# Sums of two adaLN vectors on VectorE, 256 columns of both at a time, instead of 32-column products

## The chip, the cores and the metric

The kernel runs on one core of one Trainium2 chip. Time is that of the device for one execution, in microseconds (us). Five engines work beside each other and wait for one another by semaphores: TensorE (PE in the profile, its weight loads PEld), VectorE (DVE), ScalarE (ACT), GpSimd (POOL) and SyncE (SP), which here issues the loads of weights.

## The reference

Two blocks of two layers each work on 256 tokens of 1024 features, the first one with 256 context tokens beside them. What matters here is how the layers of the first block are steered: a vector `c` (and a second one, `c_ctx`, for the context) gives shift, scale and gate through one product with `w_ada` of 1024 x 3072.

```python
sc = jax.nn.silu(c)                 # 1024 numbers
sc_ctx = jax.nn.silu(c_ctx)         # 1024 numbers
for l in range(2):
    shift, scale, gate = split((sc @ w_ada[l] + b_ada[l]), 3)
    shift_c, scale_c, gate_c = split(sc_ctx @ w_ada[l] + b_ada[l], 3)
    h  = rmsnorm(x, norm_w) * (1 + scale) + shift
    hc = rmsnorm(ctx, norm_w) * (1 + scale_c) + shift_c
    ...                             # h @ w_in; mLSTM, difference attention and Fourier branch; merge
    x = x + gate * merge(...)
    ctx = ctx + gate_c * merge(...) # first layer only
```

So each column of `w_ada` is summed twice, once with the weights of `silu(c)` and once with those of `silu(c_ctx)`. The second block (window attention, block attention, MLP) has only one such vector for each layer.

## The kernel before

All big products run in float32, with each operand split into a high and a low part and three products (high x high, high x low, low x high) for each 128 rows of the contraction. Weights come as tiles of 128 x 1024 numbers (512 KB) through nine slots w, loaded from a queue of SP. For each tile ACT makes the high part and DVE the low part (`w<-w,w`), and PE then works on it for some 24 products of 512 columns. Of raw tiles, that is loaded and not yet split or summed, five may wait (`NR`).

The kernel's program is written out at build time by a planner. It walks through the products stage by stage (in the first layer: the projections W, U, cz and bz, then the merge stages M00 to M31, four weight tiles each) and keeps a clock for each engine. Between two products it puts in "side work": attention steps, evacuations, splits and the adaLN sums, when by its clocks their operands are there and ACT and DVE are not too far ahead. A stage can name groups of side work that must be done before it starts (`need=`): U3 needs the attention's groups of its first unit, bz0 those of the second. What is left of them is then put in all at once by `plan.drain`, with no products between. Engines execute in the order that the planner wrote.

Tiles of `w_ada` are loaded between the other weight tiles (`stream.ada(..., rate=...)`). A chunk is 512 columns of `w_ada`, in four tiles. The chunks that matter here are

- the four of `mod1`, scale and shift of the second layer of the first block, loaded between the tiles of the stages from U1 on (in the trace their products with `stat` stand between 468.7 and 638.1), in use from layer 1 on;
- the two of the first layer's gates, group `gate0`, loaded from W24 on. They are applied by `ada_gate`, whose `use` waits for `have`, which says that the slot for the finished gates has come free (at the start of stage M30, in `pre_out`).

Each such tile goes to PE: four products of 32 x 256 with a block of `stat`, in which the two vectors stand among zeros (`p<-w,stat`), summed in PSUM over the chunk's four tiles. ACT copies the sum to the tile `acc`. For `mod1` (`ada_feat`) two small products against constants (`p<-cst,acc` of 128x8) bring the sums into columns, and for the gates (`ada_gate`) products of `acc` with a constant (`p<-acc,cst`) spread the row over all 128 partitions; DVE adds these to the bias that a DMA has put in place.

Chunks with one vector alone (the second block's, and the first block's last gate) already take another way, `ada_vec`: DVE multiplies the tile by a column of `stat` and adds it to `acc`, 512 columns at a time; PE sums over the partitions by a product with ones (`ada_rows`), ACT copies, a transpose makes columns, and DVE adds the bias. The tile `acc` has one buffer: `G("acc", 1)`.

Of the kernel before, what the change touches and what calls it, by code (L numbers as in the profile page):

```python
# [11 lines left out]
ALU = mybir.AluOpType  # L12
# [41 lines left out]
CALM, CALM2 = 750, 750  # L54
# [7 lines left out]
C_ID, C_SC, C_CS, C_Z, C_AL = 0, 128, 136, 652, 655  # L62
# [7 lines left out]
INF = float("inf")  # L70
# [3 lines left out]
class Bank:  # L74
# [3 lines left out]
    def __init__(self, *deps, n=1):  # L78
        self.deps, self.n = deps, n
# [503 lines left out]
def _build(tc, a, out, es):  # L583
    plan = Planner(lambda i: lp.tile([128, 512], F32, name=f"p{i}", tag=f"p{i}"), 3, 4)
# [38 lines left out]
    def expect(group, n=1):  # L623
        plan.pending[group] = plan.pending.get(group, 0) + n

    def fin(group):
        plan.pending[group] -= 1


    cst = cp.tile([128, NCST], F32, name="cst")  # L630
# [4 lines left out]
    ones = cp.tile([128, 128], F32, name="ones")  # L635
# [4 lines left out]
    def C(name, i=0, n=1):  # L640
        o = _COLS[name] + i
        return col[:, o:o + n]


    stat = cp.tile([128, 60], F32, name="stat")
# [34 lines left out]


    def ada_run(ch, stream):
        if ch["vec"] is not None:
            return ada_vec(ch, stream)

        def gen(_):
            prev = ch["prev"]
            over = lambda: INF if prev and not prev.get("over") else 0.0
            first = lambda: INF if prev and not prev.get("summed") else 0.0

            def there(q):
                return lambda: plan.gate([stream.raw[ch["idx"][q]]]) if q in ch["idx"] else INF
            ps = yield Bank(there(0), first)
            for q in range(4):
                if q:
                    yield [there(q)]
                elif "pre" in ch:
                    ch["pre"]()
                i = ch["idx"][q]
                r = stream.raw.pop(i)  # L700
                for par in range(2):
                    for half in range(2):
                        g = 32 * (2 * par + half)
                        nc.tensor.matmul(ps[g:g + 32, 0:256], stat[:, 4 * (2 * q + par):4 * (2 * q + par) + 32],
                                         r[:, 512 * par + 256 * half:512 * par + 256 * half + 256],
                                         start=(q == 0), stop=(q == 3))
                stream.drop(r)
            ch["summed"] = True
            yield [ps, over]
            sb = G("acc", 1)[:, 0:256]  # L710
            nc.scalar.activation(sb, ps[:, 0:256], AF.Copy)
            plan.release(ps)
            yield from ch["use"](sb)
            ch["over"] = True
        return gen

    def ada_vec(ch, stream):
# [31 lines left out]
            ch["over"] = True  # L749
        return gen  # L750

    def chunk(w, group, use, vec=None):
        expect(group)
        ch = dict(w=w, group=group, vec=vec)
        if isinstance(use, tuple):
            use, ch["pre"] = use
        ch["use"] = use
        return ch
# [44 lines left out]
    def ada_row(dst, brow):  # L803
# [9 lines left out]
            nc.gpsimd.dma_start(dst.rearrange("a (f n) -> (a f) n", f=4), acc[0:128:32, 0:128])  # L813
        return use, start

    def ada_gate(dsts, brow, wait):

        ds = {}

        def load():  # L820
            if not ds and wait() == 0.0:
                ds.update(dsts())
                for d in ds.values():
                    nc.gpsimd.dma_start(d, brow.to_broadcast([128, 512]))

        def use(sb):
            yield [wait]
            load()
            for m, d in ds.items():
                ps = yield Bank(sb, d)  # L830
                for half in range(2):
                    o = C_SC + 4 * half + m
                    nc.tensor.matmul(ps[:, 256 * half:256 * half + 256], cst[:, o:o + 1].to_broadcast([128, 128]), sb,
                                     start=True, stop=True)
                yield [ps]
                nc.vector.tensor_tensor(d, ps, d, ALU.add)
                plan.release(ps)
        return use, load

    class Mod:  # L840

        def __init__(self, group, w, bias, b0, norm, ms):
            self.ok = [0] * 4
            self.m = self.A = None
            self.ms, self.norm, self.group = ms, norm, group
            one = len(ms) == 1
            use = ada_cols if one else ada_feat
            self.chunks = [chunk((lambda q, c=c: w(c, q)), group,  # L850
                                 use((lambda c=c: self.dst(c)), C(bias, b0 + 4 * c, 4), lambda c=c: self.fin(c)),
                                 ms[0] if one else None)
                           for c in ((0, 2, 1, 3) if one else range(4))]

        def dst(self, c):
            n = len(self.ms)
            if self.A is None:
                b = 2 if n > 1 else 4
                self.A = cp.tile([128, n, 8], F32, name=f"modA{n}", tag=f"modA{n}", bufs=b)
                self.S = cp.tile([128, n, 8], F32, name=f"modS{n}", tag=f"modS{n}", bufs=b)  # L860
                if n > 1:
                    self.m = cp.tile([128, 2, 8, 3], F32, name="mod", tag="mod")
            if n > 1:
                return self.m[:, :, 2 * c:2 * c + 2, :]
            return (self.S, self.A)[c // 2][:, 0, 4 * (c % 2):4 * (c % 2) + 4]

        def fin(self, c):

            if self.m is not None:
                k0, n, qs = 2 * c, 2, (c,)  # L870
            else:
                k0, n, qs = 4 * (c % 2), 4, (2 * (c % 2), 2 * (c % 2) + 1)
            k = slice(k0, k0 + n)
            for q in qs:
                self.ok[q] += 1 if self.m is None else 2
            if self.ok[qs[0]] < 2:
                return
            for i, m in enumerate(self.ms):
                scale = self.A[:, i, k] if self.m is None else self.m[:, 1, k, m]
                nc.vector.scalar_tensor_tensor(self.A[:, i, k], scale, 1.0, C(self.norm, k0, n), ALU.add, ALU.mult)  # L880
                if self.m is not None:
                    nc.vector.tensor_copy(self.S[:, i, k], self.m[:, 0, k, m])
# [74 lines left out]
    stream = Stream(nc, plan, lambda i, dt: wp.tile([128, 1024], dt, name=f"w{i}", tag=f"w{i}"), mm, ada_run)  # L957
# [430 lines left out]
    def layer1(l, X, norm, ada_next, begin_out, on_token):  # L1388
# [317 lines left out]
        have = lambda: 0.0 if "gate" in st else INF  # L1706
        for c in range(2):
            gemm(W(24 + c), 8, 512, feats(vq, nx), ev_mc(c), pre=None if c else pre_mc,
                 need=() if c or last else ("cc",))
            if c == 0 and not last:  # L1710
                stream.ada(*[chunk((lambda q, c=c: a["wada"][l, 4 + c, q]), f"gate{l}{c}",
                                   ada_gate((lambda c=c: {m: st["gate"][:, m, 512 * c:512 * c + 512]
                                                          for m in range(2)}),
                                            a["bgate"][l:l + 1, 512 * c:512 * c + 512], have)) for c in range(2)],
                           front=True, rate=RATE["gate"])
                stream.ada(rate=RATE["mid"])
        if last:
# [142 lines left out]
    do(start_0)  # L1860


    mod1 = Mod("ada1", lambda c, q: a["wada"][1, c, q], "bada1", 0, "norm1", (0, 1))
    norm1 = Norm("h1", range(4), mod1, lambda t: 0 if t in (0, 3) else 1)

    def begin_1():
# [380 lines left out]
    n0, b0 = norm_of(0, mods[0][0])  # L2247
# [8 lines left out]
def _chunks(w, width=512):  # L2256

    import numpy as np
    K, N = w.shape
    kq = 1024 // width  # L2260
    v = w.reshape(K // (128 * kq), kq, 128, N // width, width).transpose(3, 0, 2, 1, 4)
    return np.ascontiguousarray(v).reshape(N // width, K // (128 * kq), 128, 1024)
# [31 lines left out]
def layout(inp):  # L2294
    import numpy as np
    g = {k: np.asarray(v) for k, v in inp.items()}
    d = {}
# [17 lines left out]
    win, wg, wmix, wada = [], [], [], []  # L2315
    win2, wkv2, wo2, wout2, wup2, wdn2, wada2 = [], [], [], [], [], [], []
    for l in range(2):
# [18 lines left out]
        w = g["w_in"][l]  # L2336
        o = np.cumsum([0, 512, 512, 1024, 16, 1024, 1024, 1024, 1024, 1024, 1024, 1024, 1024, 3072])
# [16 lines left out]
        w = g["w_ada"][l]  # L2354

        w = np.concatenate([w[:, :2048].reshape(1024, 2, 4, 256).transpose(0, 2, 1, 3).reshape(1024, 2048), w[:, 2048:]], 1)
        wada.append(_chunks(w))
        w = g["w_in_2"][l]
        o = np.cumsum([0, 512, 128, 128, 512, 512, 512, 1024, 1024])
        p = [w[:, o[i]:o[i + 1]] for i in range(8)]  # L2360
# [33 lines left out]
```

## Time and profile before

| | |
|---|---|
| runs | 2292.09, 2286.84, 2292.26 us; median 2292.09 |
| the profiled execution | 2286.09 us |
| its span in the profile | 2284.3 us |
| PE busy | 2242.7 us, 98% |
| PEld (weight loads, beside PE) | 1901.5 us, 83% |
| DVE busy | 1484.3 us, 65% |
| ACT busy | 1107.0 us, 48% |
| POOL busy | 269.0 us, 12% |

Busy time is the time in which at least one instruction of an engine was under way. Instructions of one engine overlap a little, so that the time from one start to the next is what counts in a row of them. A product in full float32 leaves two records, and so the profile's counts for these are twice those of the program.

### The profile page before, as it was taken

Reading aid. Unit: us, or ns where it says so; the run is one execution under the profiler, and the core shown is the slowest. Engines: PE = TensorE matmul, PEld = TensorE weight load, DVE = VectorE, ACT = ScalarE, POOL = GpSimd, SP = SyncE. Lnnn points to the kernel's source line nnn. Section 1 sums busy time; section 2 is a strip of 40 time slices with the busy share of each in tenths; the row PEclk is TensorE's granted clock in tenths of the full one; section 3 lists DMA queues with packets and bytes.
Section 4 is the critical chain, followed back from the end, with each engine's and each line's share of the span. In section 5 each row is a group of like instructions: output and inputs, shape, how many; then the busy total and the mean of one; then the engine's idle time right before and its main releaser. Section 6 shows DMA issues by size and latency. Waiting matters only on the chain. (4 is left out here: it accounts for less than half of the span.)

```text
span 2284.3 us, 34929 instructions
## 1 busy us (share of the span) xinstructions
PE 2242.7 (98%) x13228; PEld 1901.5 (83%) x13228; DVE 1484.3 (65%) x2856; ACT 1107.0 (48%) x2125; POOL 269.0 (12%) x439
## 2 busy tenths in 40 slices
PE   8999999999999999999999999999999999999999
PEld 6877888877777877878898888997998987798987
DVE  4667744457676734686975877678666656758554
ACT  4345322235565423435542556556655645656653
POOL 1012000014121000010200322003000002100000
PEclk9999999999999999999999999999999999999999
DMA  7443443353323453465674423464354564345454
GB/s 291 148 152 107 133 162 120 129 171 115 102 93 102 139 193 123 146 203 196 227 266 138 145 90 120 164 206 151 103 188 168 181 213 161 113 139 207 153 193 148
DMA packets 99913, 359.79 MB, mean 158 GB/s; under 512 B 11960, under 2 KB 12272, under 8 KB 99744
## 3 DMA queue, kind: packets, MB, share of 16 engines
q1 hardware_dynamic: 96192, 348.34, 44.9%
q0 software_dynamic: 3552, 9.22, 1.6%
q8 instruction: 104, 1.70, 0.3%
q14 instruction: 65, 0.53, 0.1%
HBM read 354.31 MB, written 3.20 MB: 157 GB/s over the span
## 5 line engine op out<-in xcount | busy, mean ns | idle before, releaser
L318 PE MATMUL mm<-h,w 128*128 128x256 f32 (+1 forms) x4048 | 819.4, 319 | 2.0 <-ACT qr L318 1.0
L318 DVE TENSOR_TENSOR w<-w,w 128x1024 fp32r<-128x1024 f32 x452 | 552.5, 1222 | 401.2 <-ACT w L318 354.3
L318 ACT ACTIVATE w<-w 128x1024 fp32r<-128x1024 f32 x461 | 486.6, 1058 | 667.0 <-PE mm L318 598.7
L318 PEld LDWEIGHTS mm<-h,w 128*128 128x128 f32 x4048 | 602.8, 190 | 61.2 <-issue 13.8
L318 PE MATMUL mm<-w,h 128*128 128x512 f32 (+1 forms) x1584 | 472.0, 392 | 10.3 <-DVE w L318 7.3
L318 PE MATMUL mm<-hl,w 128*128 128x512 f32 (+1 forms) x1040 | 354.2, 341 | 0.0
L318 PEld LDWEIGHTS mm<-w,h 128*128 128x128 f32 x1584 | 286.3, 190 | 79.4 <-DVE w L318 11.7
L318 PE MATMUL mm<-s,w 128*128 128x256 f32 (+1 forms) x1536 | 256.7, 326 | 0.6 <-DVE s L318 0.6
L318 PEld LDWEIGHTS mm<-s,w 128*128 128x128 f32 x1536 | 224.1, 190 | 25.3 <-issue 3.0
L318 PE MATMUL mm<-w,s 128*128 128x512 f32 x996 | 240.1, 391 | 0.0
L318 PE MATMUL mm<-w,hl 128*128 128x512 f32 (+1 forms) x608 | 231.5, 381 | 0.0
L318 PEld LDWEIGHTS mm<-w,s 128*128 128x128 f32 x996 | 186.2, 188 | 38.5 <-issue 0.4
L318 PEld LDWEIGHTS mm<-hl,w 128*128 128x128 f32 x1040 | 197.4, 190 | 20.8 <-issue 2.9
L318 DVE SCALAR_TENSOR_TENSOR acc<-w,stat,acc 128x512 f32<-128x512 f32 x192 | 143.7, 748 | 47.2 <-DMA w<-in_wada_dram 40.7
L318 PEld LDWEIGHTS mm<-w,hl 128*128 128x128 f32 x608 | 114.8, 189 | 22.2 <-DVE hl L318 0.2
L318 ACT ACTIVATE s<-mm 128x512 f32<-128x512 f32 (+2 forms) x142 | 67.3, 481 | 63.1 <-PE mm L318 62.9
L318 PE MATMUL p<-s 64*128 64x256 f32 (+3 forms) x464 | 85.7, 390 | 3.0 <-DVE s L318 1.5
L318 POOL TENSOR_TENSOR qrs<-qrs,mhalf 128x8 f32<-128x8 f32 (+2 forms) x48 | 83.0, 1729 | 4.0
L318 POOL TENSOR_SCALAR ls<-ls 128x1 f32<-128x1 f32 x72 | 26.3, 365 | 389.6 <-ACT l1a L318 147.1
L318 PE MATMUL mm<-s,s 128*128 128x512 f32 x252 | 67.8, 389 | 0.0
L318 PEld LDWEIGHTS p<-s 64*128 64x128 f32 (+1 forms) x464 | 47.0, 186 | 23.5 <-issue 6.3
L318 DVE TENSOR_REDUCE ls<-p 128x1 f32<-128x512 f32 (+1 forms) x96 | 52.8, 593 | 12.1 <-PE p L318 11.9
(317 smaller groups left out, 2443.8 us busy)
## 6 DMA issues: line engine op xcount, KB each, us to landing
w<-in_win_dram SPq DMA_DIRECT2D x272, 512.0 KB, 3.5
w<-in_wada_dram SPq DMA_DIRECT2D x144, 512.0 KB, 3.8
w<-in_wmix_dram SPq DMA_DIRECT2D x64, 512.0 KB, 3.5
w<-in_wup_dram SPq DMA_DIRECT2D x64, 512.0 KB, 3.6
w<-in_wdn_dram SPq DMA_DIRECT2D x64, 512.0 KB, 3.5
w<-in_wo_dram SPq DMA_DIRECT2D x16, 512.0 KB, 3.5
w<-in_wout_dram SPq DMA_DIRECT2D x16, 512.0 KB, 3.6
s<-in_x_dram SPq DMA_DIRECT2D x4, 512.0 KB, 7.9
```

The lines of the kernel that those rows point to most:

```text
L318: r = f(*a, **k)
```

## The change

The six chunks named above are summed on DVE (`ada_two`). A chunk's four tiles are laid out anew, so that two tiles hold 256 columns in full (all 1024 rows, 128 at a time, in eight steps). For each half, 256 columns, DVE runs 16 operations of 128 x 256: the eight steps, each for both vectors, into the two halves of the one `acc` tile. After each half PE, ACT and DVE finish it: for `mod1` by `ada_cols2` (product with ones, copy, transpose, addition of the bias), for the gates by two products with ones of `acc`'s two halves and two additions of 128 x 256. A next half may start on `acc` when the one before has been read.

```diff
     def ada_run(ch, stream):
+        if ch["vec"] == (0, 1):
+            return ada_two(ch, stream)
         if ch["vec"] is not None:
             return ada_vec(ch, stream)
...
+    def ada_two(ch, stream):
...
+            yield [first]
+            if "pre" in ch:
+                ch["pre"]()
+            for half in range(2):
+                acc = ch["acc"] = G("acc", 1)
+                for q in (2 * half, 2 * half + 1):
+                    yield [there(q), acc] if q % 2 else [there(q)]
+                    r = stream.raw.pop(ch["idx"][q])
+                    for j in range(4):
+                        kt = 4 * (q % 2) + j
+                        for v in range(2):
+                            w, c, o = r[:, 256 * j:256 * j + 256], stat[:, 4 * kt + v:4 * kt + v + 1], acc[:, 256 * v:256 * v + 256]
+                            if kt:
+                                nc.vector.scalar_tensor_tensor(o, w, c, o, ALU.mult, ALU.add)
+                            else:
+                                nc.vector.tensor_scalar(o, w, c, None, ALU.mult)
+                        if j < 3:
+                            yield [acc]
+                    stream.drop(r)
+                ch["summed"] = half == 1
+                yield from ch["use"](acc, half)
+            ch["over"] = True
...
+    def ada_cols2(dst, bias, then):
+
+        def use(acc, half):
+            yield from ada_rows(acc)
+            ps = yield Bank(calm(acc))
+            transposes(ps, acc, 1)
+            yield [ps]
+            nc.vector.tensor_tensor(dst(half), ps[:, 0:128:32].rearrange("p (v f) -> p v f", v=2),
+                                    bias[:, 2 * half:2 * half + 2].unsqueeze(1).to_broadcast([128, 2, 2]), ALU.add)
...
-        def use(sb):
+        def use(acc, part):
             yield [wait]
             load()
             for m, d in ds.items():
-                ps = yield Bank(sb, d)
-                for half in range(2):
-                    o = C_SC + 4 * half + m
-                    nc.tensor.matmul(ps[:, 256 * half:256 * half + 256], cst[:, o:o + 1].to_broadcast([128, 128]), sb,
-                                     start=True, stop=True)
+                ps = yield Bank(calm(acc), d)
+                nc.tensor.matmul(ps[:, 0:256], ones, acc[:, 256 * m:256 * m + 256], start=True, stop=True)
                 yield [ps]
-                nc.vector.tensor_tensor(d, ps, d, ALU.add)
+                o = d[:, 256 * part:256 * part + 256]
+                nc.vector.tensor_tensor(o, ps[:, 0:256], o, ALU.add)
                 plan.release(ps)
...
-    mod1 = Mod("ada1", lambda c, q: a["wada"][1, c, q], "bada1", 0, "norm1", (0, 1))
+    mod1 = Mod("ada1", lambda c, q: a["wada"][1, c, q], "bada1", 0, "norm1", (0, 1), dve=True)
...
+        for c in ((4, 5), (0, 1, 2, 3))[l]:
+            d_[c] = _chunks(w[:, 512 * c:512 * c + 512], 256).reshape(4, 128, 1024)
```

Since the planner decides by its clocks, the order changes around the new steps too. Up to the first sums of `mod1`, at U0, and again from the second layer of the first block on, the order of the program is the same as before; in between, up to M31, it differs.

On PE, the start of stage U3 before (`mm<-h,w` are the last products of cz1, `mm<-w,h` the first of U3):

```order
L318 MATMUL mm<-h,w_5241 128x512
L318 MATMUL mm<-hl,w_5241 128x512
L318 MATMUL mm<-h,w_5270 128x512
L318 MATMUL mm<-w_5347,h 128x512
L318 MATMUL mm<-w_5383,h 128x512
```

U3's products follow those of cz1 at once. The same place after the change, where s and vb, l0a to l2b are operands of the attention, p PSUM tiles of side work, and w_5255 U3's weight:

```order
L318 MATMUL p_5363<-s_4108 128x256
L318 MATMUL p_5377<-cst,vb_5251 128x128 x4
L318 MATMUL p_5391<-s_3275,vb_5387 128x128 x4
L318 MATMUL p_5405<-cst,l0a 128x128 x4
L318 MATMUL p_5414<-cst,l1a 128x128 x2
L318 MATMUL p_5425<-s_3275,l0b 128x128 x4
L318 MATMUL p_5433<-s_3275,l1b 128x128 x2
L318 MATMUL p_5440<-cst,l2a 128x128 x2
L318 MATMUL p_5443<-cst,vb_5403 128x128
L318 MATMUL mm<-w_5255,h 128x512
L318 MATMUL mm<-w_5289,h 128x512
```

These are the last rows of a run of 43 PE instructions of the attention and the sums (among them `p_5443`, which reads `vb_5403`) that now stands between cz1's last product and U3's first, `mm<-w_5255,h`.

On DVE, in the same run after the change (ls are columns of the attention's softmax, w_5273 a tile of `w_ada`):

```order
L318 TENSOR_SCALAR acc<-w_5273,stat 128x256 x2
L318 SCALAR_TENSOR_TENSOR ls_5093<-ls_5093,nlam 128x1
L318 SCALAR_TENSOR_TENSOR ls_5242<-ls_5242,scol 128x2
L318 TENSOR_REDUCE ls_5243<-p_5341 128x1
L318 TENSOR_REDUCE ls_5243<-p_5342 128x1
L318 SCALAR_TENSOR_TENSOR acc<-w_5273,stat,acc 128x256 x2
L318 SCALAR_TENSOR_TENSOR vb_5251<-vb_5253,ls_5093,vb_5251 128x512
L318 SCALAR_TENSOR_TENSOR ls_5093<-ls_5093 128x1
L318 SCALAR_TENSOR_TENSOR ls_5243<-ls_5243,scol 128x2
L318 SCALAR_TENSOR_TENSOR acc<-w_5273,stat,acc 128x256 x2
L318 RECIPROCAL ls_5242<-ls_5242 128x2
L318 TENSOR_REDUCE ls_5339<-p_5362 128x1
```

Sums into acc stand between the attention's reductions and updates. Before, this run did not exist: DVE's steps of the attention stood beside products of cz0 and cz1.

On DVE, the start of stage M30 before (`s_7954` is the slot of the gates, `p_8005` to `p_8062` the four products that spread them, `w_8027` and `w_8066` low parts of the coming weights, `s_7782` the low part of the merge's result):

```order
L318 SCALAR_TENSOR_TENSOR s_7782<-s_7351,s_7781 128x512 x2
L318 TENSOR_TENSOR s_7954<-p_8005,s_7954 128x512
L318 TENSOR_TENSOR s_7954<-p_8013,s_7954 128x512
L318 TENSOR_TENSOR w_8027<-w_7901,w_8017 128x1024
L318 TENSOR_TENSOR s_7954<-p_8053,s_7954 128x512
L318 TENSOR_TENSOR w_8066<-w_7971,w_8056 128x1024
L318 TENSOR_TENSOR s_7954<-p_8062,s_7954 128x512
```

Four additions and two splits stand there. And after the change, where `s_8032` is the slot of the gates, w_7689 to w_7978 are four tiles of `w_ada`, and `w_8139` and `w_8196` low parts of M30's weights:

```order
L318 TENSOR_TENSOR s_8032<-p_8084,s_8032 128x256
L318 TENSOR_TENSOR s_8032<-p_8090,s_8032 128x256
L318 TENSOR_SCALAR acc<-w_7689,stat 128x256 x2
L318 SCALAR_TENSOR_TENSOR acc<-w_7689,stat,acc 128x256 x6
L318 SCALAR_TENSOR_TENSOR acc<-w_7774,stat,acc 128x256 x8
L318 TENSOR_TENSOR w_8139<-w_8118,w_8135 128x1024
L318 TENSOR_TENSOR s_8032<-p_8137,s_8032 128x256
L318 TENSOR_TENSOR s_8032<-p_8142,s_8032 128x256
L318 TENSOR_SCALAR acc<-w_7866,stat 128x256 x2
L318 SCALAR_TENSOR_TENSOR acc<-w_7866,stat,acc 128x256 x6
L318 SCALAR_TENSOR_TENSOR acc<-w_7978,stat,acc 128x256 x8
L318 TENSOR_TENSOR w_8196<-w_8153,w_8192 128x1024
```

Between the additions for the first half (`p_8084`, `p_8090`) and those for the second (`p_8137`, `p_8142`) now stand 16 sums and a split, and 16 more sums and a split before those for the first half of the second gate chunk (`p_8194`, which follows). On PE, `p_8137` stands 18 products behind `p_8090`.

## Rows read from the trace of the kernel before

**Rows 1.** The page: span, engines (busy, share), granted clock in slices, one group, one load.

```profile
span 2284.3 us, 34929 instructions
...
PE 2242.7 (98%) x13228; PEld 1901.5 (83%) x13228; DVE 1484.3 (65%) x2856; ACT 1107.0 (48%) x2125; POOL 269.0 (12%) x439
...
PEclk9999999999999999999999999999999999999999
...
L318 ACT ACTIVATE w<-w 128x1024 fp32r<-128x1024 f32 x461 | 486.6, 1058 | 667.0 <-PE mm L318 598.7
...
w<-in_wout_dram SPq DMA_DIRECT2D x16, 512.0 KB, 3.6
```

**Rows 2.** Windows: stretch, length, each engine's busy time (instructions), granted clock, DMA share.

```profile
630.00:660.00 30.00, 28.44 (x166) 22.26 (x163) 24.88 (x63) 19.29 (x46) 14.28 (x22) 1.00 0.25 81
...
690.00:720.00 30.00, 29.02 (x158) 21.23 (x157) 20.21 (x49) 17.08 (x44) 4.77 (x8) 1.00 0.33 107
...
900.00:930.00 30.00, 30.00 (x139) 24.38 (x138) 17.22 (x22) 8.11 (x10) 2.17 (x4) 1.00 0.62 200
...
470.00:650.00 180.00, 177.93 (x996) 134.36 (x995) 120.34 (x281) 92.33 (x208) 52.04 (x75) 1.00 0.36 118
```

**Rows 3.** List of waits, PE, 500 to 790: total, times, longest.

```profile
PE p L318 <- ACT l0a L318: 1.5, 1, 1.5
```

**Rows 4.** PE timeline at bz0's start: start, length, instruction, [idle before it, releaser].

```profile
646.42 0.39 PE L318 MATMUL mm<-w,hl 128*128 128x512 f32 x1
646.65 1.05 PE L318 MATMUL p<-s,vb 128*128 128x128 f32 x8
...
649.27 1.41 PE L318 MATMUL p<-cst,qr 128*128 128x128 f32 x8 [1.46 <-ACT l0a L318]
...
650.55 0.47 PE L318 MATMUL mm<-h,w 128*128 128x512 f32 x1
```

**Rows 5.** PE by form, whole span: busy, mean ns of one record.

```profile
L318 PE MATMUL p<-w,stat 128*32 128x256 f32 x320 | 25.6, 396 | 5.8 <-DMA w<-in_wada_dram 5.8
...
L318 PE MATMUL p<-acc,ones 128*32 128x128 f32 x208 | 11.1, 285 | 0.0
...
L318 PE MATMUL p<-cst,acc 128*128 128x128 f32 x16 | 4.3, 271 | 0.0
L318 PE MATMUL p<-cst,acc 128*128 128x8 f32 x32 | 4.2, 238 | 0.5 <-ACT acc L318 0.5
```

**Rows 6.** PE timeline, one group of 32-column products.

```profile
559.30 0.64 PE L318 MATMUL p<-w,stat 128*32 128x256 f32 x8
```

**Rows 7.** DVE by form: the nearest operations to the new ones, and a split.

```profile
L318 DVE TENSOR_TENSOR w<-w,w 128x1024 fp32r<-128x1024 f32 x452 | 552.5, 1222 | 401.2 <-ACT w L318 354.3 <-PE p L318 32.8 <-PE mm L318 5.6
...
L318 DVE SCALAR_TENSOR_TENSOR l1a<-l1b,ls,l1a 128x256 f32<-128x256 f32 x8 | 3.8, 481 | 0.2
...
L318 DVE TENSOR_SCALAR l1a<-l1a,ls 128x256 f32<-128x256 f32 x3 | 1.1, 352 | 0.1
```

**Rows 8.** DVE timeline at two places.

```profile
512.39 0.47 DVE L318 SCALAR_TENSOR_TENSOR l1a<-l1b,ls,l1a 128x256 f32<-128x256 f32 x1
512.79 0.15 DVE L318 SCALAR_TENSOR_TENSOR ls<-ls 128x1 f32<-128x1 f32 x1
...
686.97 0.76 DVE L318 TENSOR_REDUCE ls<-p 128x1 f32<-128x256 f32 x2
```

**Rows 9.** PE products with stat, 440 to 660: first and last start.

```profile
L318 PE MATMUL p<-w,stat x128: 377/379/403, 468.7 to 638.1; 128*32 128x256 f32 x128
```

**Rows 10.** PE timeline at M30's start, where the gates are applied.

```profile
911.72 0.84 PE L318 MATMUL mm<-w,s 128*128 128x512 f32 x3
...
919.50 5.82 PE L318 MATMUL mm<-w,s 128*128 128x512 f32 x24
925.17 1.02 PE L318 MATMUL p<-acc,cst 128*128 128x256 f32 x4
```

**Rows 11.** List of waits, PE, 895 to 1000.

```profile
PE mm L318 <- DVE w L318: 1.1, 1, 1.1
```

More of the change, by code (lines that the diff above doesn't have):

```diff
@@ L750, in ada_vec, with gen, first, there @@
         return gen
+    def ada_two(ch, stream):
+        def gen(_):
+            prev = ch["prev"]
+            def first():
+                if prev and not prev.get("over"):
+                    return INF
+                return max(plan.used.get(k, (0, ""))[0] for k in plan._keys(prev["acc"])) if prev and "acc" in prev else 0.0
+            def there(q):
+                return lambda: plan.gate([stream.raw[ch["idx"][q]]]) + CALM2 if q in ch["idx"] else INF
+            yield [first]
[20 more added lines that the diff above has]
+            ch["over"] = True
+        return gen
     def chunk(w, group, use, vec=None):
@@ L814, in ada_row @@
         return use, start
+    def ada_cols2(dst, bias, then):
[6 more added lines that the diff above has]
+                                    bias[:, 2 * half:2 * half + 2].unsqueeze(1).to_broadcast([128, 2, 2]), ALU.add)
+            plan.release(ps)
+            if half:
+                then()
+        return use
     def ada_gate(dsts, brow, wait):
@@ L840, in _build, with __init__ @@
     class Mod:
-        def __init__(self, group, w, bias, b0, norm, ms):
+        def __init__(self, group, w, bias, b0, norm, ms, dve=False):
             self.ok = [0] * 4
+            self.dve = dve
             self.m = self.A = None
@@ L848, in __init__, with dst @@
             one = len(ms) == 1
-            use = ada_cols if one else ada_feat
+            use = ada_cols if one else ada_cols2 if dve else ada_feat
             self.chunks = [chunk((lambda q, c=c: w(c, q)), group,
-                                 use((lambda c=c: self.dst(c)), C(bias, b0 + 4 * c, 4), lambda c=c: self.fin(c)),
-                                 ms[0] if one else None)
+                                 use((lambda *h, c=c: self.dst(c, *h)), C(bias, b0 + 4 * c, 4), lambda c=c: self.fin(c)),
+                                 ms[0] if one else ms if dve else None)
                            for c in ((0, 2, 1, 3) if one else range(4))]
-        def dst(self, c):
+        def dst(self, c, half=None):
             n = len(self.ms)
@@ L860, in dst @@
                 self.S = cp.tile([128, n, 8], F32, name=f"modS{n}", tag=f"modS{n}", bufs=b)
-                if n > 1:
+                if n > 1 and not self.dve:
                     self.m = cp.tile([128, 2, 8, 3], F32, name="mod", tag="mod")
+            if self.dve:
+                return (self.S, self.A)[half][:, :, 2 * c:2 * c + 2]
             if n > 1:
@@ L867, in fin @@
         def fin(self, c):
-            if self.m is not None:
+            if self.m is not None or self.dve:
                 k0, n, qs = 2 * c, 2, (c,)
@@ L874, in fin @@
             for q in qs:
-                self.ok[q] += 1 if self.m is None else 2
+                self.ok[q] += 1 if self.m is None and not self.dve else 2
             if self.ok[qs[0]] < 2:
@@ L1713, in layer1 @@
                                                           for m in range(2)}),
-                                            a["bgate"][l:l + 1, 512 * c:512 * c + 512], have)) for c in range(2)],
+                                            a["bgate"][l:l + 1, 512 * c:512 * c + 512], have), (0, 1)) for c in range(2)],
                            front=True, rate=RATE["gate"])
@@ L2356, in layout @@
         w = np.concatenate([w[:, :2048].reshape(1024, 2, 4, 256).transpose(0, 2, 1, 3).reshape(1024, 2048), w[:, 2048:]], 1)
-        wada.append(_chunks(w))
+        d_ = _chunks(w)
+        for c in ((4, 5), (0, 1, 2, 3))[l]:
+            d_[c] = _chunks(w[:, 512 * c:512 * c + 512], 256).reshape(4, 128, 1024)
+        wada.append(d_)
         w = g["w_in_2"][l]
```

## The prediction

> **What bounds the kernel now.** I read the page first. TensorE (PE) is busy 2242.7 of 2284.3 us, VectorE (DVE) 1484.3, and the granted clock stands at the top digit, that is at the 2.4 GHz level, in every slice [rows 1]. So the kernel ends when PE ends, and only 41.6 us of PE idle time is there to win. An edit pays if it takes work from PE, and costs where it makes PE wait.
>
> Next I read the windows of the stretch that the change touches. From 900 to 930 PE is busy 30.00 of 30 us. It idles 1.56 us from 630 to 660 and 0.98 us from 690 to 720 [rows 2], about 2.5 together. DVE is busy 20 to 25 of 30 us in the attention part (630 to 720) and 17 where the merge runs [rows 2]. So DVE has room on average, between 5 and 13 us in each 30.
>
> The average hides one place. The list of waits has PE standing 1.46 us (1.5 there) for ACT's l0a [rows 3]. The timeline shows the spot: at the start of bz0 the last product stands at 646.42, then come only matmuls of side work until 650.55 [rows 4]. That is a drain: bz0 needs a finished group, and `plan.drain` puts all that is left of it in a row, with no product between. There PE is as fast as the chain over DVE, ACT and POOL, and not as fast as itself. At that place the order has 14 PE instructions (2.0 us of work) and 13 on DVE (4.2 us). The difference is 2.2, the measured wait 1.46. I use this pair below to scale.
>
> **The change part by part.**
>
> *PE, removed.* Six chunks (four of the second layer's scale and shift, two of the first layer's gates) of four tiles each lose one group of four 32-column products per tile. The trace has 320 records of such products, 25.6 us, in 40 groups of 8 [rows 5], so 0.64 each, as the one in the timeline at 559.30 [rows 6]. 24 groups give 24 x 0.64 = 15.4 us. Each of the four mod chunks also loses two small products against constants: 32 records of 8 chunks, 4.2 us, so 0.53 a chunk [rows 5], 2.1 in all.
>
> *PE, added.* Each mod chunk now makes its columns twice, once per half: 8 groups of four products of acc with ones, 0.43 each (208 records, 26 groups, 11.1 us), and 8 transposes at 0.27 (16 records, 4.3 us) [rows 5]: 3.4 + 2.2 = 5.6 us. The gates' products keep their count. Net on PE: 5.6 - 17.5 = **-12 us**. PE is the bound, so this counts in full where nothing waits.
>
> *ACT and small steps.* Six copies of p to acc go and eight come; the gates' four additions on DVE become eight of half the width, and a mod chunk's small DVE steps keep about their number. ACT is busy 1107.0 of 2284.3 us [rows 1], and the copies lie beside products. Zero; where such a copy is late in a drain, it is in the drain's term.
>
> *DVE, added.* A half is 16 operations of 128x256: 14 multiply-adds with one scalar, 2 multiplies. By form the nearest rows say 0.48 and 0.35 each [rows 7]; but the timeline has the next operation starting 0.40 after such a multiply-add (512.39 to 512.79), while its record lasts 0.47 [rows 8]. For the multiply I take 0.27, the record less the same overlap. So 14 x 0.40 + 2 x 0.27 = 6.2 us a half, and 7.4 by whole records. Twelve halves make 74 us, at most 89. On average this fits. The mod chunks are 8 halves, 50 us. Before, the 128 records of their products lie between 468.7 and 638.1 [rows 9], and in the 180 us from 470 to 650 DVE was busy 120.3 and PE 177.9 [rows 2]. With 50 more DVE comes to 170 of 180: nearly as loaded as PE, and no longer able to run ahead of it.
>
> *Terms from drains.* In the order after, the sums stand between the attention's DVE steps, and the attention comes late. Four places now have a run of side work between two products, priced as PE work / DVE work at starts apart: in U1's second tile 1.1 / 5.2, at cz0's start 1.9 / 6.0, at U3's start 43 PE instructions 5.8 / 46 on DVE 13.9, at bz0's start 53 PE 6.7 / 51 on DVE 16.4. As an example, U3's 13.9 are twelve sums (4.5), six reductions (2.6: 0.34 for each of four of 256 columns, whose pair lasts 0.76 [rows 8], 0.6 for two of twice the width), four vector updates of 512 and 256 columns (2.1), two steps on e (1.2), three scalings out of PSUM (1.0) and the small ones. Before, U3 had no such run: its first product followed cz1's last. The differences are 4.1, 4.1, 8.1 and 9.7 us. I take off 0.75 each, as bz0 taught (2.2 against 1.46): 3.4 + 3.4 + 7.3 + 9.0 = 23. The 2.5 us that PE idled there before [rows 2] are among them, so **+21**. The bounds: half of it, if the sums fall into waits that DVE has anyway; or more, if ACT and POOL steps between them leave DVE idle.
>
> *Terms from the gates.* Their sums wait for `have`, set at M30's start, because acc has one buffer: only the first half can be summed ahead, and the next one may start when PE has read the last. Before, M30's first product started at 911.72, and 24 products between two gate products ran from 919.50 to 925.17, so 0.236 each, 5.5 to 5.7 a tile [rows 10]. The one wait in the stretch is 1.1 for a weight [rows 11]. I walk from M30's start after the change: the gate's second product of the first half (p_8090) stands 24 + 6 products in, at 7.8. Then DVE needs two evacuations and 16 sums, 8.2 to 14.4. PE comes to p_8137 after 18 products, at 11.9, and waits 2.6. The low part of the next weight (1.22 us [rows 7]) is queued behind the sums on DVE. It lands at 15.6, when PE needs it at once. The second gate's first half runs 16.0 to 22.2, PE is there at 21: 1.2. Its second half is mixed with M30's own evacuations, 1 to 3 more. Total 5 to 8 and up to 11 with 7.4 a half; **+7**. Bounds 0 (if these sums are quicker than any row here) and 11.
>
> *A rule weighed.* The multiply-add's row has the next one starting 0.07 before its record ends [rows 8]. The Trainium skill, VectorE: DVE Perf Modes, section "The DRAIN you can't avoid", says that the next operation does not start until the pipe of the one before is empty. By that rule a half would be 7.4, M30's term 11, and the 18 sums in the four runs 1.4 us more: +21 for the change instead of +16. The sum here goes by the row.
>
> *DMA.* The bytes are the same. Waiting gate tiles hold raw places until their half is summed, so M30's third tile is requested late, about 2 us of PE work ahead instead of 29. Loading and splitting it is hidden behind the same sums (the wait counted above); without those it would cost 3.6 us of landing and 1.06 of ACT [rows 1] less those 2, about 3. Zero more.
>
> *Sum:* -12 + 21 + 7 = **+16 us**. The profiled execution took 2286.09 us (span 2284.3), the median of the runs is 2292.09 and the quickest 2286.84. So 2302 on the profile's basis and 2308 on the median's; I give 2308.
>
> **The rivals.**
> - *DVE keeps up (chance 0.16).* The runs of sums fall into gaps that the attention leaves DVE, half of the 23 is seen, M30 costs 4: 11.5 - 2.5 + 4 - 12 = +1, 2293 us. For it: DVE's 120 of 180 [rows 2]. Against it: U3's drain has 13.9 us of DVE work in a row whatever came before.
> - *PE's saving alone (0.09), the other side.* The sums stand early enough that PE finds every result ready and no drain grows: -12, 2280 us. It decides if DVE does a multiply-add of 256 columns in about 0.25 us: then U3's run falls by 1.8, the mod part to 33 us and M30's half to 4, less than the 18 products that cover it. The rows of 0.47 to 0.48 [rows 7, 8] speak against it.
> - *Sums that hold up chains (0.13).* Each POOL or ACT step of a drain starts late, since the DVE step ahead of it stands behind sums; DVE then idles for their answer too. bz0's run has 17 POOL and 24 ACT instructions. 3 us in each of the four drains is +12: 2320 us. For it: the one measured drain waited for ACT, not DVE [rows 3].
> - That the products stay on PE is excluded: in the order PE has 96 products of 32 columns fewer and 64 instructions fewer in all.
>
> **How the numbers follow.** The forecast, drains and gates together, has 0.62. Its own range is 2298 to 2316 (drains 12 to 27, gates 4 to 11). The three rivals have the other 0.38. The range of 8 in 10 leaves out the case of 2280 and the far half of 2320: 2289 to 2320. A measurement of this kernel tells about 0.3%, here 2285.2 to 2299.0. Faster: the second rival and little of the first, 0.10. Within: most of the first and the lower end of the forecast, 0.17. Slower: 0.73.
>
> **What would show it.** Right: in the profile after, PE busy falls by 12 to about 2231, PE's idle time grows from 41.6 to some 70, and the list of waits names "p" products waiting for ACT or DVE in the attention stretch (8 to 9 us each at two places near 620 and 645) and "p" or "mm" waiting on DVE's acc and w around 915 to 935, 2.6 and 1.2 among them. The windows between 510 and 660 have DVE at 27 or more of 30. A pair of sums starts 0.80 apart. Wrong: PE still busy 30 of 30 there, or sums under 0.3 us, or waits for a DMA in M30, or idle time that sits outside 470 to 960, where the order is the same as before.

## The result

| | before | after |
|---|---|---|
| median | 2289.47 us (2285.6 to 2292.26, 4 runs) | 2306.34 us (2303.24 to 2309.48, 4 runs) |
| ratio | | 1.0075, 95% interval 1.0061 to 1.0089 |
| the profiled execution's span | 2284.3 us | 2305.0 us |

The change makes the kernel about 17 us slower; +16 was forecast, 2308 against the median of 2292.09 that was known then. Of the page of the changed kernel, the span, the engines and the granted clock (before: [rows 1]):

```profile
span 2305.0 us, 34849 instructions
...
PE 2247.6 (98%) x13092; PEld 1909.8 (83%) x13092; DVE 1553.4 (67%) x3048; ACT 1108.8 (48%) x2127; POOL 269.8 (12%) x439
...
PEclk9999999999989999999999999999999999999999
```

DVE has 69 us more, as forecast (74). But PE's busy time did not fall by 12: it rose by 4.9, and idle time went only from 41.6 to 57.4. The digit 8 in the clock's row (the slice from 634 to 691 us) is where to look.

The two programs are the same ahead of U0 and behind M31, so I compared stage by stage, from the first product of a stage to that of the next. The windows of before, for cz0 and cz1, U3, bz0 to W23, M30 and M31, and one stage of layer 1 (columns as in [rows 2]):

```profile
549.28:612.87 63.59, 63.59 (x362) 48.15 (x360) 44.61 (x107) 32.07 (x79) 17.51 (x25) 1.00 0.32 101
612.87:650.55 37.68, 36.12 (x213) 26.99 (x211) 25.63 (x65) 22.01 (x54) 9.51 (x18) 1.00 0.33 111
650.55:773.75 123.20, 122.22 (x664) 96.06 (x662) 90.61 (x200) 70.49 (x174) 21.18 (x38) 1.00 0.32 107
...
911.72:961.47 49.75, 49.75 (x234) 40.78 (x232) 30.40 (x51) 18.55 (x36) 6.39 (x14) 1.00 0.43 140
...
1015.11:1041.27 26.16, 24.63 (x118) 19.17 (x117) 18.25 (x60) 7.76 (x10) 3.00 (x7) 1.00 0.55 183
```

And of the changed kernel, the same five:

```profile
542.11:617.47 75.36, 68.43 (x358) 52.52 (x357) 66.69 (x169) 37.45 (x88) 15.48 (x25) 0.93 0.32 105
617.47:668.38 50.91, 46.74 (x249) 34.40 (x248) 40.16 (x110) 29.00 (x76) 18.05 (x28) 0.87 0.20 63
668.38:787.66 119.28, 118.78 (x634) 93.57 (x634) 86.68 (x186) 68.94 (x168) 18.48 (x34) 1.00 0.33 107
...
919.73:977.05 57.32, 52.17 (x225) 41.19 (x224) 49.64 (x104) 19.22 (x36) 6.07 (x14) 0.97 0.48 158
...
1030.67:1061.40 30.73, 29.04 (x118) 22.07 (x116) 18.42 (x63) 7.76 (x10) 2.30 (x6) 0.83 0.50 160
```

The first two stages grew by 11.8 and 13.2 us, the third shrank by 3.9, and M30 and M31 grew by 7.6. U0 to U2 took 5.3 less, since attention work of theirs now stands later (the two profiles are 1.9 us apart at 460 and 7.2 at cz0's start); W24 to M21, which have the gates' products no more, 5.9 less. Together 17.5. The profiles' spans are 20.7 us apart, because of what lies where the programs are the same: 1.9 us in the changed kernel's favour ahead of U0, and 5.1 against it behind M31. The third to last number of each row is the granted clock: 0.93, 0.87 and 0.97 in three of the stages where before had 1.00. The last row is a stage in which both programs are the same: 4.6 us longer at a clock of 0.83; more on it at the end.

Inside the drain ahead of U3, the changed kernel's PE timeline:

```profile
601.01 0.39 PE L318 MATMUL mm<-h,w 128*128 128x512 f32 x1
601.33 0.96 PE L318 MATMUL p<-s 64*128 64x512 f32 x6
...
606.26 1.00 PE L318 MATMUL p<-s 64*128 64x256 f32 x5 [1.48 <-DVE modA L318]
...
612.12 2.07 PE L318 MATMUL p<-s,vb 128*128 128x128 f32 x8 [0.75 <-ACT vb L318]
...
617.47 0.70 PE L318 MATMUL mm<-w,h 128*128 128x512 f32 x2
```

cz1's last products start at 601.01, U3's first at 617.47, and from 601.33 on there is only side work: 16.1 us, for which the order's DVE work was priced at 13.9. The row at 612.12 is eight matmuls in 2.07 us; eight of the same form took 1.05 before [rows 4]. So PE runs at half its clock there, and its busy time counts double. Windows of 3 us show when that began:

```profile
600.00:603.00 3.00, 2.29 (x13) 1.30 (x11) 2.93 (x5) 2.31 (x4) 0.00 (x0) 1.00 0.45 127
603.00:606.00 3.00, 1.04 (x3) 0.46 (x3) 2.97 (x7) 0.37 (x1) 0.00 (x0) 0.85 0.57 223
606.00:609.00 3.00, 1.61 (x8) 1.02 (x8) 2.96 (x13) 1.63 (x4) 0.00 (x0) 0.50 0.01 3
609.00:612.00 3.00, 2.10 (x9) 1.41 (x9) 3.00 (x14) 1.73 (x5) 0.00 (x0) 0.50 0.00 0
```

PE idled 0.71 and 1.96 us of 3, and then the clock was 0.50, the 1.2 GHz level, from about 605 to 615. On DVE in the same drain:

```profile
607.11 0.75 DVE L318 TENSOR_REDUCE ls<-p 128x1 f32<-128x256 f32 x2
607.78 0.87 DVE L318 SCALAR_TENSOR_TENSOR acc<-w,stat,acc 128x256 f32<-128x256 f32 x2
608.57 0.74 DVE L318 SCALAR_TENSOR_TENSOR vb<-vb,ls,vb 128x512 f32<-128x512 f32 x1
...
609.37 0.87 DVE L318 SCALAR_TENSOR_TENSOR acc<-w,stat,acc 128x256 f32<-128x256 f32 x2
610.16 0.16 DVE L318 RECIPROCAL ls<-ls 128x2 f32<-128x2 f32 x1
610.24 0.73 DVE L318 TENSOR_REDUCE ls<-p 128x1 f32<-128x256 f32 x2
```

DVE has no gap in these rows. A pair of sums takes 0.79 (607.78 to 608.57), so 0.40 a sum as forecast, and the pairs stand between the reductions and the small steps on ls. PE's waits here name ACT (0.95 us for l0a, 0.75 for vb), but ACT itself had waited 2.94 us for DVE's ls ahead of l0a. The windows of the two whole runs of side work, U3's and bz0's, show which engine sets the pace:

```profile
601.33:617.47 16.14, 10.75 (x54) 8.01 (x54) 15.21 (x49) 8.28 (x24) 1.12 (x3) 0.68 0.29 98
650.42:668.38 17.96, 13.81 (x66) 9.51 (x66) 15.32 (x48) 11.45 (x30) 9.64 (x15) 0.62 0.09 30
```

DVE is busy for 15.2 and 15.3 us of them; PE idles 5.4 and 4.2 us, and does the rest of its side work at a mean clock of 0.68 and 0.62. By form, over the whole program (before: [rows 7]):

```profile
L318 DVE SCALAR_TENSOR_TENSOR acc<-w,stat,acc 128x256 f32<-128x256 f32 x168 | 70.9, 476 | 4.8 <-DMA w<-in_wada_dram 4.7
...
L318 DVE TENSOR_SCALAR acc<-w,stat 128x256 f32<-128x256 f32 x24 | 7.3, 346 | 10.3 <-DMA w<-in_wada_dram 10.3
```

A record lasts 0.476, and the next starts 0.08 before it ends. By the Trainium skill's rule that was weighed in the prediction (VectorE: DVE Perf Modes, section "The DRAIN you can't avoid") a pair would be 0.95, if the end of a record is taken for the empty pipe; the trace does not agree with it here. The same section adds that an operation that is not held starts earlier; the 0.79 fits that, but no run here shows that it is the reason.

At M30 the changed kernel's PE timeline shows its waits (before: [rows 10]), and DVE's what they are for:

```profile
933.17 1.10 PE L318 MATMUL p<-acc,ones 128*128 128x256 f32 x4 [1.49 <-DVE acc L318]
935.41 0.49 PE L318 MATMUL mm<-w,s 128*128 128x512 f32 x1 [1.13 <-ACT w L318]
936.67 6.89 PE L318 MATMUL mm<-w,s 128*128 128x512 f32 x23 [0.77 <-DVE w L318]
```

```profile
929.78 3.64 DVE L318 SCALAR_TENSOR_TENSOR acc<-w,stat,acc 128x256 f32<-128x256 f32 x9
935.39 1.23 DVE L318 TENSOR_TENSOR w<-w,w 128x1024 fp32r<-128x1024 f32 x1 [1.97 <-ACT w L318]
```

PE waits 1.49 for the second half's sums, then 1.13 for the high part and 0.77 for the low part of the third weight tile. In the DVE rows the sums end at 933.42, and then DVE itself idles 1.97 for ACT's high part: the tile was loaded late (asked for at 925.38, it landed 8.8 us later). The clock fell behind these waits: from 936.67 to 943.40 it was 0.78, and the 23 products there took 6.73 us where 0.236 each, as before [rows 10], makes 5.4.

### The profile page after: what moved, and what is told of

Read it like the earlier page. It is cut to its first block, busy times and chain, and to the rows that moved or that the text cites. A ratio compares the mean times of both kernels' runs of the same rounds, so it can differ in the third digit from the quotient of the medians.

```text
span 2305.0 us, 34849 instructions
## 1 busy us (share of the span) xinstructions
PE 2247.6 (98%) x13092; PEld 1909.8 (83%) x13092; DVE 1553.4 (67%) x3048; ACT 1108.8 (48%) x2127; POOL 269.8 (12%) x439
## 3 DMA queue, kind: packets, MB, share of 16 engines
q8 instruction: 103, 1.69, 0.3%
## 5 line engine op out<-in xcount | busy, mean ns | idle before, releaser
L318 DVE SCALAR_TENSOR_TENSOR acc<-w,stat,acc 128x512 f32<-128x512 f32 (+1 forms) x360 | 214.6, 621 | 47.6 <-DMA w<-in_wada_dram 41.3
```

The costliest lines, as they stand in the source:

```text
L318: r = f(*a, **k)
```

## The experiments

Each was timed against the kernel before on the same chip; the ratios are to that.

**The scale and shift alone.** The gates go back to PE (old `ada_gate`, old layout for them):

```diff
-  ada_gate(..., have), (0, 1)) for c in range(2)]
+  ada_gate(..., have)) for c in range(2)]
...
-        for c in ((4, 5), (0, 1, 2, 3))[l]:
+        for c in ((), (0, 1, 2, 3))[l]:
```

> Only the second layer's scale and shift are summed on DVE; the first layer's gates stay on PE as before. Theory (the cost sits in the attention part: sums delay its DVE steps, so that PE stands in the drains at U3 and bz0 and its clock falls there): from the stages of the two profiles this part is worth -5.2 + 11.8 + 13.2 - 3.9 = about +16 us, so about 2305 us against 2289.5 of before. Rival (each half on DVE costs alike, wherever it stands): 8 of 12 halves of +17, so about +11, 2301 us.

2306.9 us, ratio 1.0087 (1.0073 to 1.0100): +20 by the ratio and +18.7 by the medians (2288.21 for the kernel before), against an expected +16. Its windows for the three attention stages:

```profile
544.50:620.20 75.70, 68.77 (x358) 52.85 (x357) 67.01 (x169) 37.45 (x88) 15.48 (x25) 0.93 0.32 105
620.20:670.72 50.52, 46.37 (x249) 34.67 (x248) 39.81 (x109) 28.58 (x75) 17.86 (x27) 0.86 0.20 63
670.72:789.92 119.20, 118.71 (x633) 93.54 (x634) 86.63 (x186) 69.12 (x170) 18.38 (x34) 1.00 0.33 107
```

They are those of the changed kernel within 0.4 us, so this part brings the whole of the attention's loss, and the rival of a like cost for each half (1.0048) falls outside the interval. Of what goes beyond the 16, 3.6 us stand in its profile in the stage of W24, where a gate's product waited 2.6 us for its DMA.

**The gates alone.**

```diff
-    mod1 = Mod("ada1", ..., (0, 1), dve=True)
+    mod1 = Mod("ada1", ..., (0, 1))
...
-        for c in ((4, 5), (0, 1, 2, 3))[l]:
+        for c in ((4, 5), ())[l]:
```

> Only the first layer's gates are summed on DVE; scale and shift of the second layer stay on PE as before. Theory: 8 groups of 32-column products go (5.1 us), M30 gains about 5 us of waits and some 2 us of lower clock, so about +2 us, 2291 us, with the waits on acc and w at M30 as in the changed kernel. Rival (each half costs alike): 4 of 12 halves of +17, about +6, 2295 us. Rival (M30's waits came from scale and shift, by loads or splits that were late): no waits at M30 and about -5 us, 2285.

2287.36 us, ratio 0.9997 (0.9989 to 1.0006): no difference, where +2 was expected; both rivals, +6 and -5, fall outside the interval. Windows of U3 and of M30 and M31:

```profile
610.51:648.19 37.68, 36.12 (x212) 26.98 (x211) 25.63 (x66) 21.99 (x54) 9.50 (x18) 1.00 0.33 111
903.03:960.10 57.07, 52.23 (x225) 41.37 (x224) 49.63 (x104) 19.25 (x36) 6.03 (x14) 0.97 0.48 159
```

U3's stage is that of before to 0.01 us, and M30 and M31 have the 57 us of the changed kernel. So M30's waits belong to the gates, and eat up what the gates' products saved.

**A quarter of the sums.** Of each tile only the first of four steps is summed; three quarters of the sums are left out (and with them the points between steps at which the planner could put in other work), everything behind them stays:

```diff
                         for v in range(2):
+                            if j:
+                                continue
...
-                        if j < 3:
-                            yield [acc]
```

> The changed kernel with six of the eight steps of each half's sum left out (of each of its two tiles only the first 128 rows are summed), so 4 operations a half instead of 16; all loads, products with ones, copies, transposes and additions stay. What it leaves out: three quarters of the adaLN sums of the six chunks. Theory: DVE's time for the sums is the cause; with 1.5 us a half the drains and M30's waits shrink to about those of before, and PE's saved 12 us show: about 2279 us (2275 to 2284). Rival (the cause is the longer chain behind each half, ones, copy, transpose, addition, or that acc has one buffer): stays above 2290.

2276.2 us, ratio 0.9952 (0.9938 to 0.9966), 11 us less than before. Of its page the engines, and windows of cz0 and cz1, U3, bz0 to W23, M30 and M31:

```profile
PE 2231.9 (98%) x13092; PEld 1901.0 (84%) x13092; DVE 1500.2 (66%) x2904; ACT 1105.7 (49%) x2127; POOL 268.3 (12%) x439
```

```profile
546.97:610.41 63.44, 63.44 (x360) 49.75 (x358) 50.46 (x122) 33.72 (x85) 16.86 (x27) 1.00 0.34 109
610.41:643.14 32.73, 32.73 (x194) 25.06 (x193) 23.01 (x64) 19.89 (x54) 5.87 (x12) 1.00 0.33 112
643.14:762.20 119.06, 119.06 (x638) 93.77 (x637) 90.95 (x197) 69.72 (x167) 25.18 (x40) 1.00 0.34 111
893.93:945.81 51.88, 49.86 (x225) 40.52 (x224) 35.70 (x68) 19.19 (x36) 6.22 (x14) 1.00 0.51 174
```

The drains are gone (63.44 and 32.73 against 63.59 and 37.68 of before), and PE's busy time has fallen, by 10.8. So the 12 us of PE are real, the loss is the time of the sums on DVE, and not the longer chain behind each half. M30 and M31 keep 2 us of waits.

**Products put into the drains.** Where the planner foresees a wait of PE ahead of U3 and bz0 (d is a PSUM tile taken for it):

```diff
+                for g in st["need"]:
+                    while plan.pending.get(g, 0):
...
+                        t = min(plan.at(i) for i in plan.ev + plan.pri + plan.flight)
+                        for _ in range(int((t - plan.t[PE]) // 218) if t < INF else 0):
+                            nc.tensor.matmul(d[:, 0:128], self.ones, self.ones, start=True, stop=True)
+                        plan.side(force=True)
             for g in st["need"]:
                 plan.drain(g)
```

> The changed kernel with products of ones with ones put into the drains ahead of U3 and bz0, wherever the planner's clocks foresee that PE waits, 59 products of 128 columns, some 13 us of PE time that nobody reads; otherwise the same work. Theory (the waits lower the granted clock, and the lower clock costs time of its own, in and behind the drains): the clock stays at 1.00 there and the kernel comes out 4 to 9 us quicker than the changed one, about 2300 us, while DVE's run of work in the drains keeps its length. Rival (the drains are paced by DVE and the clock there costs nothing): 2306 or some us more, since the products stand ahead of real ones.

2305.67 us, ratio 1.0076 (1.0063 to 1.0088), the same as the changed kernel. Its windows for the three attention stages:

```profile
545.59:619.99 74.40, 72.46 (x429) 57.81 (x427) 65.93 (x167) 37.31 (x88) 15.44 (x25) 1.00 0.32 107
619.99:669.23 49.24, 47.46 (x298) 36.60 (x295) 40.80 (x111) 28.84 (x76) 18.73 (x29) 1.00 0.21 65
669.23:787.96 118.73, 118.73 (x634) 93.56 (x634) 86.60 (x186) 68.90 (x168) 18.00 (x33) 1.00 0.33 107
```

The clock is 1.00 now, and the stages are shorter by 1.0, 1.7 and 0.6 us only. My theory, that the lower clock costs 4 to 9 us, falls: most of PE's slow time lay inside waits for DVE. Up to 3 us of it may be real; the runs can't tell this from nothing. The products that were put in hold little up in their turn: between 600 and 671 us DVE's steps on ls waited 0.7 us for PE here, and 2.5 in the changed kernel.

**Attention first.** The planner offers attention steps ahead of these sums:

```diff
-            for it in self.pri + self.flight:
+            for it in sorted(self.pri + self.flight, key=lambda i: bool(i.get("low"))):
```

> The changed kernel, but the planner offers the attention's steps before the sums of the six chunks (before: sums first). Theory (DVE has no room between U0 and bz0, 170 of 180 us, so whoever goes first the other is late): the drains at U3 and bz0 get shorter, but sums fall back, their raw tiles keep their places, and PE waits for weights instead: still over 2295, about 2300 us. Rival (only the order hurts): the drains go back to those of before (3.9 us at bz0, none at U3) and the kernel comes to 2280 to 2288.

2298.92 us, ratio 1.0045 (1.0028 to 1.0062). Windows of the same three stages:

```profile
542.11:603.65 61.54, 61.23 (x328) 47.79 (x327) 46.76 (x108) 31.62 (x79) 16.22 (x25) 1.00 0.27 86
603.65:647.13 43.48, 39.49 (x223) 28.76 (x221) 37.47 (x105) 24.27 (x66) 8.39 (x15) 1.00 0.25 80
647.13:782.51 135.38, 126.19 (x667) 95.84 (x666) 110.14 (x255) 71.89 (x170) 25.34 (x40) 0.99 0.36 123
```

The first two stages get 21 us shorter than in the changed kernel, and the third 16 longer, with 9.2 us of idle time of PE. Who goes first matters for some 7 us of the 17; the rest only changes its place. The way expected was wrong in part: PE waited there for the sums and for ACT's steps, and only 0.8 us for a weight.

**Scale and shift later.**

```diff
-            stream.ada(*ada_next, front=True, rate=RATE["conv"])
...
             bz(0, b(1))
+            stream.ada(*ada_next, front=True, rate=1.25)
             bz(1)
...
-            stream.ada(rate=RATE["mix"])
+            pass
```

> The changed kernel with the tiles of the second layer's scale and shift loaded and summed later, from bz1 on (one for every 1.25 weight tiles) instead of from U1 on (one for every 1.5); the gates as in the change. Theory (the place hurts, not the sums as such): U1 to bz0 lose their drains, and the merge stages have DVE room (14 to 19 of 30 us busy); some waits may come where the last attention units stand, around W22. About 2285 us (2280 to 2295), M30's waits as in the change. Rival (sums cost alike wherever they stand, or the loads, now denser, hold PE up): 2300 or more.

2293.42 us, ratio 1.0016 (1.0005 to 1.0026): 13 us better than the change. U3's stage, and the DVE sums that still stand in the attention, by tile:

```profile
600.76:646.14 45.38, 41.36 (x214) 31.29 (x213) 35.99 (x88) 26.87 (x69) 16.39 (x27) 0.88 0.26 82
```

```profile
L318 DVE SCALAR_TENSOR_TENSOR acc<-w,stat,acc x30: 735/744/754, 468.7 to 628.2; 128x512 f32<-128x512 f32 x30
```

The stream filled the free places with the next chunks in its list, those with one vector: 30 sums of 512 columns (0.744 each) and two multiplies between 468 and 628. U3's stage stays 7.7 us over before's. So sums on DVE hurt there whoever's they are, and the experiment undid only part of what it meant to.

**The gates ahead.** Gates alone on DVE; all four halves are summed before use, into l0b, l1b, l2b (the attention's, free by then) and acc:

```diff
-                acc = ch["acc"] = G("acc", 1)
+                acc = ch["acc"] = (G(ch["ahead"][half], 1) if ch["ahead"] else G("acc", 1))
...
-                yield from ch["use"](acc, half)
+                if ch["ahead"]:
+                    accs.append(acc)
+                else:
+                    yield from ch["use"](acc, half)
+            for half, acc in enumerate(accs):
+                ch["over"] = True
+                yield from ch["use"](acc, half)
...
```

> Only the gates on DVE (scale and shift on PE), and their four halves are summed ahead into four tiles of their own (three that the attention has done with, and acc), so that at M30 only the products with ones, the additions and the copies are left. Theory (M30's waits come from acc's one buffer): the waits on acc and w at M30 go, M30's stage falls from 57 to about 50 us, and the kernel comes to about 2281 us, 6 under the version with the gates alone. Rival (M30 waits for late weight tiles, whose places the gate tiles held): little change, 2285 to 2288.

2280.81 us, ratio 0.9960 (0.9945 to 0.9974). M30 and M31:

```profile
904.17:953.14 48.97, 48.97 (x225) 40.69 (x224) 34.31 (x63) 18.14 (x35) 6.37 (x14) 1.00 0.43 142
```

No wait is left, neither for the sums nor for the late tile: 48.97, less than before's 49.75, at full clock. The one buffer was the cause, and this version beats both kernels.

**Both.** Scale and shift from bz1 on, gates ahead (the last two edits together).

> Scale and shift summed from bz1 on, and the gates summed ahead into four tiles. Theory: both costs of the change go and PE's saved 12 us stay, about 2278 us (2274 to 2286), the quickest correct version. Rival (sums only trade places with other waits): 2288 or more.

2286.9 us, ratio 0.9982 (0.9971 to 0.9993): a little quicker than before, but 6 us slower than with the gates alone, and above the expected 2274 to 2286. M30 and M31 are at 49.01, and U3's stage at 44.92, as in the experiment before last. In the profiles layer 1 starts at 956.52, against 953.14 with the gates alone: 3.4 of the 4.4 us between their spans (2285.3 and 2280.9).

**No sums in the attention at all.** As above, with a rate of one adaLN tile for every 99 other tiles from U1 to bz0, so that none is loaded there:

```diff
             unit(0, "s0", ("C",))
+            stream.ada(rate=99)
```

> As the last version (scale and shift summed from bz1 on, gates summed ahead), but with no adaLN tile at all between U0 and bz1: in the last version the chunks with one vector took the free places there, 32 sums of 512 columns from 468 to 628 us. Theory (any sums on DVE beside that attention draw out the drains): bz0's stage falls from 44.9 to at most the 37.7 of before, no clock below 1.00 there, and the kernel comes to 2272 to 2280 us. Rival (the tiles left out there have to be summed later and cost as much in the second layer): 2284 to 2290.

2301.18 us, ratio 1.0058 (1.0046 to 1.0070), 11 us over even the rival's range. Windows of U3 and of the stage of layer 1 shown above, and PE in the latter:

```profile
603.22:635.61 32.39, 32.39 (x182) 26.17 (x180) 21.54 (x51) 18.60 (x50) 7.60 (x15) 1.00 0.21 66
1001.44:1035.57 34.13, 30.14 (x120) 22.75 (x117) 20.60 (x67) 7.67 (x11) 1.65 (x3) 0.80 0.40 128
```

```profile
1016.83 0.79 PE L318 MATMUL mm<-w,h 128*128 128x512 f32 x1 [3.99 <-DVE w L318]
```

The half about the attention held: U3 takes 32.39 at full clock, and layer 1 starts at 948.08 in the profile, against 961.47 before. The other half was the rival's: the 16 tiles that are left out come later, and from layer 1 to the end 28 us are lost, in this stage 8, with a wait of 3.99 for a weight's low part. PE's waits for low parts on DVE add up to 16.4 us in this whole profile and to 7.6 in that of before. That the later sums cause them is likely, but no run here separates it.

## Why the prediction was right, and where not

- **PE's 12 us.** Right: 11 appear when the sums are mostly left out. Its sign in the profile was wrong (PE busy at 2231, idle at 70), since I priced PE's work at full clock and the clock fell where PE waited. For the same reason PE idled 5.4 and 4.2 us in the two long drains, where 8 to 9 each were forecast.
- **The sum's time.** Right: 0.40 forecast and measured, start to start; so the drains and the 69 us follow.
- **Drains, +21.** Right as a net size. The attention's stages lost 15.8, and PE had 6.7 of its 12 less work there: 22.5. By place, the four runs of side work took 4.7, 4.8, 16.1 and 18.0 us, 43.6, where the forecast's DVE prices less 0.75 each say 38.5. The surplus of 5 stands in the last two. In U3's, DVE was busy for 15.2 us where the order was priced at 13.9, and idled only 0.9. In bz0's it was busy for 15.3 (priced 16.4) and idled 2.6, nearly all of it for PE's side products, which ran at the lower clock. So of the third rival, DVE idle for ACT's and POOL's answers, the two long runs show 0.7 us, a wait for POOL in U3's.
- **M30, +7.** Right in size, +7.6, and in place, shown twice, with gates alone and by summing ahead; but the parts differ, so the close match is in part luck. PE's waits add up to 5.2 in the two stages, the first of them 1.5 instead of 2.6. Two terms were missed. I set the late load at zero, but DVE itself stood 1.97 us for that tile, a form of the wait for a DMA that was named as a sign of being wrong. And I walked at full clock, while behind the waits it was 0.78: 1.3 us there, where PE is the bound.
- **DVE at 27 of 30 us from 510 to 660.** Only from 540 to 570 (29.5); elsewhere 22.8 to 25.6. PE, too, was busy for all 30 us from 570 to 600, which was named as a sign of being wrong. DVE isn't full on average even here; it is the chain in the drain that is.
- **The rivals.** That DVE keeps up (2293), that PE's saving stands alone (2280) and that held-up chains add 12 us (2320) are excluded by the interval, which means 2303 to 2310 us on the median of before. The rule that was weighed (+21) lies just outside it too; the 0.40 from start to start speaks against it more plainly.

What stays open: whether the lower clock in the drains costs 3 us or nothing, and whether any order of the sums of scale and shift wins; the three that were tried did not reach the version that leaves them on PE.

## What to carry to other kernels

Work that is moved from the bounding engine to one with a third of its time free costs nothing only where nobody waits for that engine. So look at the runs of dependent steps in which the bounding engine already waits for the other one, for there each moved operation is paid nearly in full. Before moving sums of this kind, look where their buffer comes free; summing ahead into dead tiles turned a change worth nothing into 0.4%. And a stream that is told to leave a stretch fills it with what is next in line, or owes it later.

## What was not expected of the hardware

PE's busy time is no measure of its work when the clock changes: it rose by 4.9 us while its work fell by about 12. A lower clock cost some 3 us at most in the drains (the version with products put in), since PE waited there anyhow. Where PE is the bound it does cost: in the stage of layer 1 above, with the same program and a like wait (1.53 us before, 1.69 after), the clock stayed at 1.00 in one execution and was 0.83 in the other, and the stage took 26.16 and 30.73 us. Of the other profiles, the versions with the gates alone and with products put in had 26.2 at full clock there, the one with attention first 26.35 at full clock behind a wait of 1.70, and the one with a quarter of the sums 30.69 at 0.83 behind a wait of 1.60. So one wait of 1.5 to 1.7 us may or may not be followed by a lower clock, and the length of the wait does not tell which; it is worth 4.3 to 4.6 us. The clock is a part of what single executions of the same kernel differ by: of the runs of the kernel before with a clock on record, the five under 2285 us had a mean granted clock of 0.997 to 0.999, and the seven over 2291.5 us 0.993 to 0.995.
